# Row products of a batched diagonal in two large VectorE instructions instead of sixteen small ones

## The chip, the cores and the metric

The kernel runs on one core of a Trainium2 chip. The metric is the device time of one execution in microseconds (us), as a median of several executions; the profile describes one of them, and its span is about 2 us shorter than the time. The two kernels are called "before" and "changed".

VectorE (DVE in the profile) is the compute engine that multiplies and sums here. Loads and the output are moved by 16 DMA engines while VectorE works; each moves its part of a transfer in packets, and the trace has 16 landing records for a transfer (768 for the 48 transfers of before). It has landed when the last of the 16 engines has delivered its part: in before the last record of the first y load came at 22.57 us, and the first product started at 22.68.

## The reference

```python
B, N, D = 8, 4096, 512                      # x, y: float32 (B, N, D)
gram = np.matmul(x, y.transpose(0, 2, 1))
diag = np.diagonal(gram, axis1=1, axis2=2)  # = sum over d of x[b,n,d] * y[b,n,d]
diag = diag - diag.max(axis=-1, keepdims=True)
exp = np.exp(diag)
out = exp / exp.sum(axis=-1, keepdims=True) # softmax over the 4096 rows of a batch
```

Only the diagonal is wanted, so the kernel needs one dot product of 512 elements per row. It must read 134.2 MB and does little arithmetic on them.

## The kernel before

A batch has 4096 rows, 32 on each of 128 partitions. It is loaded in two half batches of 16 rows a partition; there are 16 half batches, n = 0 to 15, each with an x and a y tile of 4 MB in a pool of three buffers.

```python
R, H, P = 32, 16, 128                       # rows of a batch and of a half batch on a partition; partitions
io = ctx.enter_context(tc.tile_pool(name="io", bufs=3))

def load(b, r0, parts):                     # x and y on the same queue, piece by piece
    xt = io.tile([P, H, D], f32, ...); yt = io.tile([P, H, D], f32, ...)
    o = 0
    for n in parts:
        nc.sync.dma_start(out=xt[:, o:o+n, :], in_=xv[b, :, r0+o : r0+o+n, :])
        nc.sync.dma_start(out=yt[:, o:o+n, :], in_=yv[b, :, r0+o : r0+o+n, :])
        o += n
    return xt, yt

def dots(b, r0, xt, yt):                    # one instruction for each row
    for k in range(H):
        c = b * R + r0 + k
        nc.vector.scalar_tensor_tensor(out=xt[:, k, :], in0=xt[:, k, :], scalar=1.0,
            in1=yt[:, k, :], op0=mult, op1=mult, accum_out=diag[:, c:c+1])

# softmax(b): 4 VectorE, 2 GpSimd, 1 ScalarE instructions and the output of 16 KB  [cut]

for b in range(B):
    for h in range(2):
        last = b == B - 1 and h == 1
        parts = [8, 4, 2, 1, 1] if last else [H]
        xt, yt = load(b, h * H, parts)
        dots(b, h * H, xt, yt)
    softmax(b)
```

## Time and profile before

| | before |
|---|---|
| time, median (3 runs) | 325.55 us (325.40 to 325.62) |
| span of the profiled run | 323.8 us |
| DMA engines busy | 90% or more from the 2nd to the 38th of 40 slices |
| data moved | 134.2 MB, 415 GB/s over the span |
| VectorE (DVE) busy | 164.4 us, 51% |
| last load has landed | 318.36 us |

These are lines of the page of before: VectorE's busy time; VectorE and the DMA engines in 40 equal slices of the span (a digit is the busy share in tenths); the queues (packets, MB, share); the chain of waits by engine; and the two largest groups of instructions (count, busy us, mean ns, then the idle time before them).

```profile
DVE 164.4 (51%) x544; ACT 4.6 (1%) x17; POOL 6.1 (2%) x20
...
DVE  0019075290944709256191742908348091571994
...
DMA  8999999999999999999999999999999999999980
...
q1 hardware_dynamic: 5760, 134.22, 96.6%
...
q14 instruction: 5, 0.04, 0.0%
...
DMA 82%; DVE 16%; issue 1%; SPq 0%; POOLq 0%; POOL 0%; DVEq 0%
...
L51 DVE SCALAR_TENSOR_TENSOR xt<-xt,yt 128x512 f32<-128x512 f32 x256 | 158.3, 687 | 144.1 <-DMA yt<-in_y_dram 144.1
L51 DVE DVE_READ_ACCUMULATOR xt<-xt,yt 128x1 f32 x256 | 21.1, 82 | 0.0
```

The loads set the time. VectorE waits 144 us for them. A row product leaves two records on VectorE, the product and the read of its accumulator. The 16% of VectorE in the chain is not a bottleneck: it is the link from the release of a buffer to the issue of the next load, and that load then stands in a queue: the one issued at 269.00 us lands 39.28 us later. The end of the chain shows it (start us, length us, what):

```profile
258.72 9.90 DVE xt L51 x32
...
268.63 0.33 SPq L43
268.96 0.04 issue
269.00 39.28 DMA yt<-in_y_dram
...
308.30 10.06 DMA yt<-in_y_dram
318.36 0.03 issue
318.40 0.04 issue
318.45 0.71 DVE xt L51 x2
```

The last y piece lands at 318.36; one row product and a softmax follow, 5.4 us to the end of the span.

**Below the page: an uneven load.** The trace also records, for each transfer, when each of the 16 DMA engines has delivered its part. Below, *lag* is the time of the last of the 16 minus the median of the 16, "middle" is that median; both are worked out from these records. Until 47 us the lag is 0.2 us. Then it rises in steps, and the second slowest engine stays within 0.3 us of the middle in all loads, so it is one engine that falls behind. The steps come where the instruction queue (q14 above) moves a packet of 8 KB; the 32 KB packet of a load that starts as the instruction packet ends takes longer than the usual 1213 ns (the median):

```
before: packets of the instruction queue, and the load packet beside each
 starts at us   takes ns   next 32 KB load packet takes ns   lag afterwards us
    47.4          332              1875                        1.0
   125.0          309              1787                        1.9
   185.5          309              1862                        2.9
   263.0          312              1869                        3.9
   322.7          493              none (the loads are over)
```

The time of an instruction packet and the lengthening of the load packet add up to 0.88 to 0.99 us, about the size of a step. The last load is complete only when the slowest engine is. 15 of 16 engines had ended by about 314.8 us; the kernel waited for the one to 318.36.

### The profile page before, as it was taken

To read this page: it belongs to the slowest core of one execution; us is meant where nothing else is said; L and a number is where in the kernel's file an instruction comes from. 1 tells how busy PE (TensorE), PEld (TensorE's weight loads), DVE (VectorE), ACT (ScalarE), POOL (GpSimd) and SP (SyncE) were. 2 spreads that over 40 slices of the span, in tenths; PEclk is the share of its full clock that TensorE was granted. 3 is DMA by queue.
4 is the path that set the end of the run, shared out by engine and by line. 5 is a ranking of instruction groups with operands and counts; after the bars stand their busy time and mean duration, and the time that the engine had idled before them with its cause. 6 is when DMAs were issued, how large, how long until landed. Compare 5 with 4: busy or idle time off the path is not lost.

```text
span 323.8 us, 727 instructions
## 1 busy us (share of the span) xinstructions
DVE 164.4 (51%) x544; ACT 4.6 (1%) x17; POOL 6.1 (2%) x20
## 2 busy tenths in 40 slices
DVE  0019075290944709256191742908348091571994
ACT  1000000000000000000000000000000000000000
POOL 0000000000000000000000000000000000000000
DMA  8999999999999999999999999999999999999980
GB/s 324 453 401 441 453 410 429 455 409 433 449 397 451 445 401 446 450 398 449 449 397 450 452 393 453 445 397 455 445 397 453 446 394 453 445 397 425 429 319 10
DMA packets 6917, 134.39 MB, mean 415 GB/s; under 512 B 1792, under 2 KB 1792, under 8 KB 2560
## 3 DMA queue, kind: packets, MB, share of 16 engines
q1 hardware_dynamic: 5760, 134.22, 96.6%
q10 hardware_dynamic: 1152, 0.13, 0.3%
q14 instruction: 5, 0.04, 0.0%
HBM read 134.22 MB, written 0.13 MB: 415 GB/s over the span
## 4 chain that ended last, share of the span: by engine, by line
DMA 82%; DVE 16%; issue 1%; SPq 0%; POOLq 0%; POOL 0%; DVEq 0%
DMA yt<-in_y_dram 82%; DVE xt L51 16%; SPq L43 0%; DVE mxp L65 0%; POOLq L114 0%; POOL mx L67 0%; DVE res L79 0%; DVE rc L78 0%; DVEq L51 0%; DVEq L79 0%; POOLq L67 0%
## 5 line engine op out<-in xcount | busy, mean ns | idle before, releaser
L51 DVE SCALAR_TENSOR_TENSOR xt<-xt,yt 128x512 f32<-128x512 f32 x256 | 158.3, 687 | 144.1 <-DMA yt<-in_y_dram 144.1
L51 DVE DVE_READ_ACCUMULATOR xt<-xt,yt 128x1 f32 x256 | 21.1, 82 | 0.0
L67 POOL PARTITION_ALL_REDUCE mx<-mxp x8 | 2.8, 350 | 308.9 <-DVE mxp L65 308.9
L71 ACT ACTIVATE res<-diag,nmx 128x32 f32<-128x32 f32 x8 | 2.6, 321 | 315.2 <-DVE nmx L69 315.2
L78 DVE RECIPROCAL rc<-ssum 128x1 f32<-128x1 f32 x8 | 1.3, 164 | 7.6 <-POOL ssum L76 7.6
L69 DVE TENSOR_SCALAR nmx<-mx 128x1 f32<-128x1 f32 x8 | 1.2, 154 | 4.3 <-POOL mx L67 4.3
L76 POOL PARTITION_ALL_REDUCE ssum<-sump x8 | 3.1, 383 | 5.8 <-ACT res L71 5.8
L79 DVE TENSOR_SCALAR res<-res,rc 128x32 f32<-128x32 f32 x8 | 1.9, 241 | 0.9
L65 DVE TENSOR_REDUCE mxp<-diag 128x1 f32<-128x32 f32 x8 | 1.5, 186 | 0.3
L71 ACT ACTIVATION_READ_ACCUMULATOR res<-diag,nmx 128x1 f32 x8 | 1.5, 186 | 0.0
L71 ACT ACT_TABLE_LOAD x1 | 1.3, 1283 | 0.7 <-PEq L103 0.7
L103 POOL MEMSET const-float32-0.0<- 128x1 f32 x1 | 0.1, 98 | 0.2 <-issue 0.2
L103 POOL MEMSET const-bfloat16-1.0<- 128x1 bf16 x1 | 0.1, 102 | 0.0
L103 POOL MEMSET const-uint8-127<- 128x1 uint8 x1 | 0.1, 101 | 0.0
L103 POOL MEMSET const-float32-1.0<- 128x1 f32 x1 | 0.1, 98 | 0.0
## 6 DMA issues: line engine op xcount, KB each, us to landing
xt<-in_x_dram SPq DMA_DIRECT2D x15, 4096.0 KB, 39.6
yt<-in_y_dram SPq DMA_DIRECT2D x15, 4096.0 KB, 48.9
xt<-in_x_dram SPq DMA_DIRECT2D x1, 2048.0 KB, 34.7
yt<-in_y_dram SPq DMA_DIRECT2D x1, 2048.0 KB, 39.3
xt<-in_x_dram SPq DMA_DIRECT2D x1, 1024.0 KB, 41.3
yt<-in_y_dram SPq DMA_DIRECT2D x1, 1024.0 KB, 43.4
xt<-in_x_dram SPq DMA_DIRECT2D x1, 512.0 KB, 35.5
yt<-in_y_dram SPq DMA_DIRECT2D x1, 512.0 KB, 27.0
```

The costliest lines, as they stand in the source:

```text
L51: nc.vector.scalar_tensor_tensor(out=xt[:, k, :], in0=xt[:, k, :], scalar=1.0, in1=yt[:, k, :], op0=mybir.AluOpType.mult, op1=mybir.AluOpT ...
L65: nc.vector.tensor_reduce(out=mxp, in_=db, axis=mybir.AxisListType.X, op=mybir.AluOpType.max)
L67: nc.gpsimd.partition_all_reduce(out_ap=mx, in_ap=mxp, channels=P, reduce_op=bass_isa.ReduceOp.max)
L69: nc.vector.tensor_single_scalar(out=nmx, in_=mx, scalar=-1.0, op=mybir.AluOpType.mult)
L71: nc.scalar.activation(out=rb, in_=db, func=mybir.ActivationFunctionType.Exp, bias=nmx, scale=1.0, accum_out=sump,)
L76: nc.gpsimd.partition_all_reduce(out_ap=ssum, in_ap=sump, channels=P, reduce_op=bass_isa.ReduceOp.add)
L78: nc.vector.reciprocal(out=rc, in_=ssum)
L79: nc.vector.tensor_single_scalar(out=rb, in_=rb, scalar=rc, op=mybir.AluOpType.mult)
L103: nc = _bacc.Bacc("TRN2", target_bir_lowering=False, num_devices=1)
```

## The change

The intent is fewer, larger VectorE instructions: one product over all 16 rows and one reduction, for the first 13 half batches. The last three stay row by row, where VectorE must be quick, and the second last is loaded in two pieces.

```diff
     def dots(b, r0, xt, yt):
+        c = b * R + r0
+        nc.vector.tensor_tensor(out=xt, in0=xt, in1=yt, op=mybir.AluOpType.mult)
+        nc.vector.tensor_reduce(
+            out=diag[:, c : c + H], in_=xt, axis=mybir.AxisListType.X, op=mybir.AluOpType.add
+        )
+
+    def dots_by_row(b, r0, xt, yt):
         for k in range(H):
             c = b * R + r0 + k
             nc.vector.scalar_tensor_tensor(
@@
-            last = b == B - 1 and h == 1
-            parts = [8, 4, 2, 1, 1] if last else [H]
+            n = 2 * b + h
+            parts = {2 * B - 2: [8, 8], 2 * B - 1: [8, 4, 2, 1, 1]}.get(n, [H])
             xt, yt = load(b, h * H, parts)
-            dots(b, h * H, xt, yt)
+            (dots_by_row if n >= 2 * B - 3 else dots)(b, h * H, xt, yt)
```

## The prediction

> **What bounds it now.** The loads. The page's slice view shows the DMA engines 90% busy or more from the second slice to the last but one, 134.2 MB at 415 GB/s over a 323.8 us span. The chain of waits is 82% "DMA yt"; the 16% of VectorE row products in it is only the link from a buffer's release to the next load's issue, and that load then queues 49 us. VectorE is busy 51%: a half batch lands every 19.4 us, its 16 row products take 9.9 us, a softmax 2.35 us every second half batch. At the end (timeline) the last y piece lands at 318.36, VectorE has then waited 0.58 us, and one row plus a softmax (5.4 us) follow.
>
> **What is less plain.** The DMA records show an uneven load. In each transfer 15 of 16 engines finish within about 0.25 us of each other; the last lags 1.0, 1.9, 2.9 and at the end 3.8 us behind the middle one. The lag steps up at 48, 126, 186 and 264 us, when the instruction queue (5 packets of 8 KB) moves a packet: the 32 KB packet beside it takes 1.8 instead of 1.21 us. I read these as VectorE's instruction fetches: some 130 VectorE records (a row product counts as two) lie between two. [...]
>
> **Removed, added, moved.** In 13 half batches 16 row products become a product and a reduction over 128x8192. [...] VectorE busy rises from 164 to about 260 us. It still fits: two half batches and a softmax are 37.1 us against 38.9 us of loading. A buffer comes free 17.4 instead of 9.9 us after landing, but about 21 us of loads are queued then. None of this is on the critical path.
>
> What is on it: VectorE's records fall from 544 to about 154, so the fetches during the loads fall from four to about one. The slow engine then ends about 1 us instead of 3.8 us behind: gain 2.8 us. Without the second-last half batch in two pieces VectorE could not use this, with its 0.58 us of slack at the end; [8, 8] starts its row products about 9.7 us earlier.
>
> **Predicted: 322.8 us**, range 321.9 to 324.5 (325.55 - 2.8, 0.8% faster). Chances: faster by over 2%: 0.02; within 2%: 0.95; slower by over 2%: 0.03.
>
> **What shows each step.**
> - Product and reduction each about 8.7 us in the groups; VectorE about 80% busy.
> - Instruction queue: 2 packets instead of 5, one of them after the last load.
> - The last y piece lands near 315.6 us, the slowest engine's lag about 1 us; VectorE waits before each last piece.
> - Packets still 1.21 us for 32 KB.
> - Loads issued about 7.5 us later after landing, with no gap in DMA.
>
> **What would make it wrong.** The reduction costs over about 10.5 us: VectorE becomes the bound, slower. The fetches are another engine's, or the lag tracks time: no gain. No fetch before the end: 322. VectorE's long two-input instructions hold back DMA writes: slower.

## The result, and the profile after

| | before | changed |
|---|---|---|
| time, median (4 runs each) | 325.52 us | 323.53 us (323.29 to 323.94) |
| span of the profiled run | 323.8 us | 321.6 us |
| VectorE busy | 164.4 us (51%) | 261.4 us (81%) |
| VectorE records counted as busy | 544 | 154 |
| instruction fetches before the last load | 4 | 1 |
| lag at the last load | 3.75 us | 1.00 us |
| last load has landed | 318.36 us | 316.13 us |

The ratio of the fast runs is 0.994, with a 95% interval of 0.9923 to 0.9958. The gain of 2.0 us is clear of the noise and far below 2%.

The same lines of the page of the changed kernel:

```profile
DVE 261.4 (81%) x154; ACT 4.6 (1%) x17; POOL 6.1 (2%) x20
...
DVE  0019979898998979979799897989979799776494
...
DMA  8999999999999999999999999999999999999991
...
q1 hardware_dynamic: 6048, 134.22, 97.5%
...
q14 instruction: 1, 0.01, 0.0%
...
DMA 63%; DVE 33%; issue 1%; SPq 1%; POOL 1%; ACT 0%; POOLq 0%; DVEq 0%
...
L50 DVE TENSOR_TENSOR xt<-xt,yt 128x8192 f32<-128x8192 f32 x13 | 113.0, 8689 | 34.5 <-DMA yt<-in_y_dram 34.5
L51 DVE TENSOR_REDUCE diag<-xt 128x16 f32<-128x8192 f32 x13 | 112.9, 8686 | 0.4
L58 DVE SCALAR_TENSOR_TENSOR xt<-xt,yt 128x512 f32<-128x512 f32 x48 | 30.0, 687 | 9.9 <-DMA yt<-in_y_dram 9.7
```

VectorE does 97 us more work, and the kernel is faster. The DMA line is as full as it was; the instruction queue has one packet instead of five in the span. The end of the chain, to be held against that of before:

```profile
265.91 8.70 DVE diag L51
274.61 0.02 issue
274.62 0.33 SPq L43
274.95 0.04 issue
275.00 30.96 DMA yt<-in_y_dram
305.95 0.02 issue
305.97 10.16 DMA yt<-in_y_dram
316.13 0.02 issue
316.15 0.71 DVE xt L58 x2
```

The last load lands 2.23 us earlier (318.36 - 316.13). The buffer of n = 12 is released at 274.6 instead of 268.6, and it does no harm: the load issued then still stands 31 us in the queue. VectorE's share of the chain has doubled, to 33%, because a half batch now holds its buffer for 17.4 us of VectorE work instead of 9.9 us and the chain passes through six of them instead of five; it costs no time at the end.

### The profile page after: what moved, and what is told of

It is laid out like the page before. It is cut to its first block, busy times and chain, and to the rows that moved or that the text cites. A ratio compares the mean times of both kernels' runs of the same rounds, so it can differ in the third digit from the quotient of the medians.

```text
span 321.6 us, 345 instructions
## 1 busy us (share of the span) xinstructions
DVE 261.4 (81%) x154; ACT 4.6 (1%) x17; POOL 6.1 (2%) x20
## 4 chain that ended last, share of the span: by engine, by line
DMA 63%; DVE 33%; issue 1%; SPq 1%; POOL 1%; ACT 0%; POOLq 0%; DVEq 0%
DMA yt<-in_y_dram 63%; DVE xt L50 16%; DVE diag L51 16%; SPq L43 1%; POOL mx L74 0%; POOL ssum L83 0%; DVE mxp L72 0%; DVE xt L58 0%; ACT res L78 0%; DVE rc L85 0%; POOLq L121 0%; SPq L44 0%; DVE res L86 0%; DVE nmx L76 0%; DVEq L50 0%
## 5 line engine op out<-in xcount | busy, mean ns | idle before, releaser
L50 DVE TENSOR_TENSOR xt<-xt,yt 128x8192 f32<-128x8192 f32 x13 | 113.0, 8689 | 34.5 <-DMA yt<-in_y_dram 34.5
L51 DVE TENSOR_REDUCE diag<-xt 128x16 f32<-128x8192 f32 x13 | 112.9, 8686 | 0.4
L58 DVE SCALAR_TENSOR_TENSOR xt<-xt,yt 128x512 f32<-128x512 f32 x48 | 30.0, 687 | 9.9 <-DMA yt<-in_y_dram 9.7
L58 DVE DVE_READ_ACCUMULATOR xt<-xt,yt 128x1 f32 x48 | 3.9, 82 | 0.0
```

The lines of the kernel that those rows point to most:

```text
L50: nc.vector.tensor_tensor(out=xt, in0=xt, in1=yt, op=mybir.AluOpType.mult)
L51: nc.vector.tensor_reduce(out=diag[:, c : c + H], in_=xt, axis=mybir.AxisListType.X, op=mybir.AluOpType.add)
```

## The experiments

Every experiment was timed over five rounds against the kernel before, except one look (all_large); no_split has four times on record. "Fetches" are the 8 KB packets of the instruction queue before the last load has landed; lag and middle are of the last load, from the landing records of the profiled run. ScE is ScalarE. Times are medians, so a row joins a median time to the landings of one run, which can be a slower one (no_split_again's profiled run took 323.56 us). all_large and the two cuts are told below; the kernel before had 325.51, 325.56, 325.61 and 325.57 us.

```
kernel           time us   fetches      lag    middle   last load
before           325.52    4            3.75   314.60   318.36
rows_pieces      326.60    4            3.68   314.60   318.27
rows_pad1        326.24    4            3.75   314.59   318.34
pad_vector       325.36    3            3.01   314.60   317.61
six_large        324.73    3            2.82   315.21   318.03
changed          323.53    1            1.00   315.13   316.13
after_again      323.43    1            0.92   315.07   315.99
pad_scalar       323.33    1 + 2 ScE    1.27   314.56   315.84
no_split         322.98    1            0.97   314.44   315.40
no_split_again   322.96    1            0.92   315.13   316.05
two_by_row       322.79    1            0.99   314.54   315.52
```

My theory: what the change saves is VectorE's instruction fetches, each of which holds back one and the same DMA engine by about 1 us. The main rivals: the pieces 8, 8 make the gain, or the larger form of the work does.

### pad_vector: put the fetches back, leave everything else

```diff
+    pad = persist.tile([P, 256], f32, name="pad")
+    for i in range(256):
+        nc.vector.memset(pad[:, i : i + 1], 0.0)
     for b in range(B):
         for h in range(2):
```

> The changed kernel plus 256 one-element memsets on VectorE before the first product, when VectorE waits for the first load anyway. Theory (what slows the last load is the number of VectorE instruction fetches): two more 8 KB packets of the instruction queue in the first 20 us, three in all before the last load; the slowest DMA engine's lag over the middle one at the last load rises from 1.0 to about 2.9 us; 325.4 us, so the whole gain is gone though the products, reductions and loads are those of the changed kernel. Rival (the gain comes from the form of the VectorE work or from the pieces 8, 8): no change, 323.5 us, lag 1.0.

Measured: 325.36 us, ratio to before 0.9994 (0.9981 to 1.0006). The gain of 2.0 us is gone but for 0.15 us. The instruction queue on its page and the end of its chain:

```profile
q14 instruction: 3, 0.02, 0.0%
```

```profile
307.53 10.07 DMA yt<-in_y_dram
317.61 0.02 issue
317.63 0.71 DVE xt L58 x2
```

The two new packets came at 6.4 and 12.0 us, while VectorE had no other work. The memsets were over at 10.05 us, the first product started at 24.5, and the products and reductions took 8689 and 8686 ns as in the changed kernel. VectorE itself stood still for 0.4 us after 61 memsets and for 1.6 us after 189, that is 128 memsets apart, with no wait that the profile shows; this fits fetches of its own. Its timeline:

```profile
0.79 1.75 DVE L91 MEMSET pad<- 128x1 f32 x61 [0.79 <-PEq L113]
2.91 3.64 DVE L91 MEMSET pad<- 128x1 f32 x128 [0.37 <-issue]
8.13 1.92 DVE L91 MEMSET pad<- 128x1 f32 x67 [1.59 <-issue]
```

Still the last load lands 1.5 us later (317.61 against 316.13), 300 us after the memsets. The middle engine ended even earlier, at 314.60 instead of 315.13; only the lag carries the delay over. It rose from 1.00 to 3.01 us, and it was 2.05 us from the first load on. This is the experiment that settles the mechanism. Beside the kernel before there is one fetch less, and the last load lands 0.75 us earlier (317.61 against 318.36); the time hides this, because from the end of the span to the end of the time 2.2 to 2.4 us went by in its runs and 1.7 to 1.8 in those of before (see the end term below).

### pad_scalar: the same number of instructions on ScalarE

```diff
+    pad = persist.tile([P, 256], f32, name="pad")
+    zero = persist.tile([P, 1], f32, name="zero")
+    nc.vector.memset(zero, 0.0)
+    for i in range(256):
+        nc.scalar.copy(out=pad[:, i : i + 1], in_=zero)
```

> The changed kernel plus 256 one-element copies on ScalarE at the start. If fetches of all engines load the same DMA engine: two more fetches, lag 2.9 us at the last load, 325.4 us. If each engine's fetches have their own DMA engine: the largest lag is about 2.0 us, the second largest about 1.0 us, time about 324.5 us. If only VectorE's fetches count: 323.5.

Measured: 323.33 us, with two more fetches at 9.7 and 21.2 us. The load packets beside them took 1459 and 1594 ns, less than the 1875 ns beside VectorE's. After these two the lag was 1.3 us; when VectorE's one fetch came at 241.6 us the largest lag stayed at 1.3 and the second largest rose to 0.9 us. So they are two different DMA engines, and only the slower of the two counts. The time is nearer to "no change" than to my 324.5. A ScalarE fetch cost about 0.55 us of lag and not 1, so the lag at the last load was 1.27 us instead of my 2.0; and what follows the end of the span took 1.9 to 2.0 us instead of the changed kernel's 2.3. Why it was shorter is open.

### six_large: half the change

```diff
-            (dots_by_row if n >= 2 * B - 3 else dots)(b, h * H, xt, yt)
+            (dots_by_row if n >= 6 else dots)(b, h * H, xt, yt)
```

> The products of the first 6 half batches in large instructions, the other 10 by row; pieces as in the changed kernel. Theory: about 395 VectorE records, so three fetches before the last load; lag 2.9 us; 324.8 to 325.4 us. Rival (gain in proportion to the half batches changed, 6 of 13): 324.6 us with a lag of about 2.7; only the number of fetches, whole ones, tells the two apart. Rival (pieces alone): 323.5.

Measured: 324.73 us, three fetches (145.1, 222.7, 293.6 us), lag 2.82. It is just under the 324.8 to 325.4 that I expected. Its profiled run was one with a late middle (see below), and 324.73 us does not tell a whole number of fetches from a gain in proportion. The count and the lag in the trace do support the theory; the time doesn't decide.

### no_split and no_split_again: without the pieces 8, 8

```diff
-            parts = {2 * B - 2: [8, 8], 2 * B - 1: [8, 4, 2, 1, 1]}.get(n, [H])
+            parts = {2 * B - 1: [8, 4, 2, 1, 1]}.get(n, [H])
```

> The changed kernel with the second-last half batch in one piece as before. What the prediction said: VectorE, with 0.58 us of slack at the end, can't use the earlier landing: about 325.0 us. Rival: that half batch lands earlier too, by the same reduced lag, so VectorE's tail moves along with it: 323.4 us, with under 1 us of wait before the last row.

Measured: 322.98 us, faster than the changed kernel. The claim of the prediction fell. The end of its chain:

```profile
305.27 10.14 DMA yt<-in_y_dram
315.40 0.03 issue
315.43 0.02 DVEq L58
315.45 0.04 issue
315.50 0.71 DVE xt L58 x2
```

VectorE had still waited 0.57 us before that last row. Since 0.5 us between calls proves little, both were run again on one chip:

> The changed kernel unaltered, beside the one without the pieces. It shows whether its 323.53 us and its middle DMA engine's later end hold. Theory: one fetch at 241 us, lag 1.0; 323.3 to 323.5 us.

> The changed kernel with the second-last half batch in one piece, on the same chip as after_again. If the pieces 8, 8 cost something: 0.2 to 0.6 us faster than after_again. If the earlier difference was one of chips or of runs: equal within 0.2 us.

Measured: 323.43 us (323.38 to 323.87) and 322.96 us (322.70 to 323.56). The medians differ by 0.47 us in the same direction as before, 0.55; the ranges overlap. The pieces don't help and appear to cost about 0.5 us. About 0.1 us of it can be reckoned from packets: a 32 KB packet took 1218.5 ns on average in before, two of 16 KB 2 x 613.5 = 1227 ns in the changed kernel, and 256 such pairs on 16 engines make 0.14 us. By the medians another 0.25 to 0.4 us lies after the end of the span: 2.3 us went by there in every run of the changed kernel and 1.8 to 2.1 without the pieces. Why is open.

### rows_pieces: only the pieces 8, 8, all products by row

```diff
-            last = b == B - 1 and h == 1
-            parts = [8, 4, 2, 1, 1] if last else [H]
+            n = 2 * b + h
+            parts = {2 * B - 2: [8, 8], 2 * B - 1: [8, 4, 2, 1, 1]}.get(n, [H])
```

> The kernel before with only the pieces 8, 8 added; every product by row. Theory: four fetches, lag 3.8 us, no gain: 325.5 to 325.9 us. Rival (the pieces make the gain): 323.5.

Measured: 326.60 us, ratio to before 1.0027 (1.0015 to 1.004). The rival falls: the pieces alone give no gain. But it is 1.0 us slower, which I had not expected, though its last load landed at 318.27, as in before. In its trace the fifth fetch starts at 322.2 us instead of 322.7, that is, during the last output, and the last output's lag is 0.92 us instead of 0.09. In before the packets of that output had ended at 322.65 us, and the fetch at 322.72 missed them by 0.07 us. Its VectorE has one record more than before (579 against 578, waits included). That made a new theory, with a test:

### rows_pad1: the kernel before with one memset more

```diff
+    pad = persist.tile([P, 256], f32, name="pad")
+    for i in range(1):
+        nc.vector.memset(pad[:, i : i + 1], 0.0)
     for b in range(B):
         for h in range(2):
```

> The kernel before with one memset on VectorE at its start and nothing else. It asks why rows_pieces was 1.0 us slower than the kernel before with its loads ending at the same time. Theory: rows_pieces has one VectorE record more (579 against 578), so the fifth fetch comes 0.5 us earlier, while the last output is written, and holds back one engine's part of it. Then one memset does the same: 326.3 to 326.7 us, lag of the last output 0.9 us instead of 0.1. Rival (the pieces cost it): 325.5.

Measured: 326.24 us, ratio to before 1.0019 (1.0006 to 1.0031). One instruction that is over in the first microseconds makes the kernel 0.6 us slower. The fifth fetch moved to 322.4 us, and the last output's lag rose to 0.81 us; the four earlier fetches and the lag of the loads are those of before. So a fetch on the last output is shown to cost about 0.6 us here, 0.1 us under what I expected. It accounts for 0.6 of the 1.0 us of rows_pieces; where the other 0.4 us comes from is not shown (the two profiled runs, 326.41 and 326.31 us, are nearly alike).

### all_large: the last three half batches in large instructions too

```diff
-            (dots_by_row if n >= 2 * B - 3 else dots)(b, h * H, xt, yt)
+            dots(b, h * H, xt, yt)
```

> The changed kernel with the last three half batches in large instructions too. The last load then lands as before, near 316 us, but VectorE begins the last product after it, 8.7 + 8.7 us, and may still be working on the half batch before: 335 to 341 us. It shows that the larger VectorE cost is hidden only as long as another load follows.

Measured in one look (a single run, state unknown): 339.9 us. The end of its chain:

```profile
305.72 9.89 DMA yt<-in_y_dram
315.62 0.02 issue
315.64 8.70 DVE xt L50
324.34 0.02 issue
324.37 8.70 DVE diag L51
333.06 0.02 issue
333.09 0.20 DVE mxp L72
```

The last load lands at 315.62, and then 17.4 us of VectorE work follow instead of 0.7. So the larger VectorE cost was hidden here only where another load followed.

### cut_120 and cut_early: take work from the slow engine

If the slow engine could be given less, the last 1 us of lag would go. My guess was that a transfer of 120 partitions is spread over 15 engines and leaves one out; which one, I did not know. The traces of cut_120 and cut_early bear out the number: the transfers of 120 and of 8 partitions have 15 and 8 landing records (a whole load has 16), besides one that comes within 1 us of the issue.

Both are changes to no_split; the lines below are those of cut_120. In cut_early the half batch n = 5 is also loaded in pieces of 15 and 1 rows.

```diff
-            nc.sync.dma_start(out=xt[:, o : o + n, :], in_=xv[b, :, r0 + o : r0 + o + n, :])
-            nc.sync.dma_start(out=yt[:, o : o + n, :], in_=yv[b, :, r0 + o : r0 + o + n, :])
+            cuts = [0, 120, P] if o == 14 else [0, P]     # cut_early: the same for row 15 of n = 5
+            for p, q in zip(cuts, cuts[1:]):
+                nc.sync.dma_start(out=xt[p:q, o:o+n, :], in_=xv[b, p:q, r0+o : r0+o+n, :])
+                nc.sync.dma_start(out=yt[p:q, o:o+n, :], in_=yv[b, p:q, r0+o : r0+o+n, :])
```

> The kernel without the pieces 8, 8, with the two loads of row 14 of the last half batch cut into partitions 0 to 119 and 120 to 127. It is a guess: if 120 partitions are spread over 15 engines [...] and the one left out is the one that VectorE's fetches slow, that engine has 1.4 us less to do and the lag at the last load goes from 1.0 to about 0.2 us: 322.4 us. If another engine is left out: lag still 1.0, about 323.1 us.

> The kernel without the pieces 8, 8, with one row of the sixth half batch (n = 5) loaded by itself, cut into partitions 0 to 119 and 120 to 127; in the middle of the run, where 20 us of loads are queued, unlike cut_120. If the engine left out by the 120 partitions is the one of VectorE's fetches: no lag after the fetch at 241 us, 322.2 to 322.5 us. If it is another one: lag 1.0 to the end, 323.0 to 323.2 us.

Measured: 325.15 and 324.80 us, both slower than no_split. It was the wrong engine. In cut_early one engine delivers its part of the last loads 0.6 us ahead of all others, and one still lags by 1.0 us. In cut_120 the slow one is among the eight of the 8-partition transfer: the last of its eight landings is 1.1 to 1.2 us behind the seventh. Why these two are some 2 us slower than no_split was not settled, but in cut_early the trace shows where: its middle engine is 0.25 us behind that of no_split before the cut row (100.23 against 99.98), 1.57 us behind just after it (130.73 against 129.16) and as far behind at the last load (315.98 against 314.44). Only the loads of the cut half batch and the next x lie between, so the cut cost the middle engine about 1.3 us. What in it does so is open.

### two_by_row: a better version

```diff
-            (dots_by_row if n >= 2 * B - 3 else dots)(b, h * H, xt, yt)
+            (dots_by_row if n >= 2 * B - 2 else dots)(b, h * H, xt, yt)
```

(on top of no_split)

> The kernel without the pieces 8, 8, with only the last two half batches by row; the third last in large instructions too. It is a search for a better version. By the numbers of all_large and no_split VectorE ends the third last half batch and its softmax at about 296.0 us, just as the second last lands (296.2), so nothing is lost at the end; the fetch stays one, since it comes at 241 us. Theory: 322.8 to 323.1 us, like no_split, lag 1.0. If fewer VectorE records alone helped in proportion, 30 fewer would be worth about 0.2 us: 322.7.

Measured: 322.79 us (322.66 to 323.02), ratio to before 0.9913 (0.9899 to 0.9927), the fastest of all, though within noise of no_split. The timeline shows how tight the hand-over is (start us, length us, engine, line, operation); in no_split VectorE had time to spare here:

```profile
295.51 0.16 DVE L85 RECIPROCAL rc<-ssum 128x1 f32<-128x1 f32 x1 [0.96 <-POOL ssum L83]
...
295.78 0.24 DVE L86 TENSOR_SCALAR res<-res,rc 128x32 f32<-128x32 f32 x1
295.93 0.69 DVE L58 SCALAR_TENSOR_TENSOR xt<-xt,yt 128x512 f32<-128x512 f32 x1
```

## Why the prediction was right or wrong

- **The bound and the hidden work: right.** VectorE rose to 81% busy, and product and reduction took 8689 and 8686 ns; the prediction's 17.4 us per half batch was my estimate for the two together. The page of before gives about the same by an estimate of its own: a reduction of 32 elements took 186 ns there and a row product of 512 took 687, so 1.04 ns for each further element, if all these instructions lie on one line, and 8.7 us for 8192. The loads stayed the bound. The slower DMA writes that the prediction names last are not seen: the usual 32 KB packet took 1213 ns (median) with VectorE 51% and 81% busy.
- **Fetches: right in number and effect.** Four fell to one, and the lag from 3.75 to 1.00 us, the predicted 2.8. pad_vector shows that this is the cause. The page shows one instruction packet and not the two I named, since the second (323.3 us) came after the span of 321.6 us. The one fetch came at 241 us, when 62 VectorE records (waits included) stood before it; in before it was 53 before the first, and 113 to 140 lay between one packet and the next.
- **The size: 2.0 us instead of 2.8.** Two terms were missing from the sum "325.55 - 2.8". The first is the end. From the end of the span to the end of the time 1.7 to 1.8 us went by in all recorded runs of before, and 2.3 us in all nine runs of the changed kernel. From the landing of the last output it was 2.61 us (325.61 - 323.00) and 3.24 (323.94 - 320.70) in the profiled runs. It was 3.2 in pad_vector too, where a fetch follows the last output as in the changed kernel, and 2.6 in two_by_row, which has none. But no_split, with such a fetch, had 2.8 and 2.9, and all_large, without, 3.0. This term stays open. It takes 0.5 to 0.6 us from the 2.8 in every run.
- **The second missing term is the middle engine, and it is one of some runs only.** In the profiled run of the changed kernel the middle ended at 315.13 instead of 314.60, so 0.53 us of the 2.75 were taken back and the landing gained 2.23. That run, 323.94 us, was the slowest of its four; the profiled runs of after_again, six_large and no_split_again, also with a late middle (315.07 to 315.21), were the slowest or second slowest of theirs. So this term says little about the median: after_again's three runs near 323.4 us are what 325.5 - 2.75 + 0.6 gives without it. It is not due to the change: no_split had a middle of 314.44 in one profiled run and 315.13 in another. In the four profiled runs with a late middle a 32 KB packet took 1216.9 to 1217.8 ns on average, without the few that took over 1400 ns; in the others 1215.0 to 1215.8, except cut_early with 1216.8. Two ns on 224 packets of an engine are 0.45 us. What makes the packets slower in some runs was not found.
- **"Without the second-last half batch in two pieces VectorE could not use this": wrong.** I took the 0.58 us of slack as fixed. But the second-last half batch lands earlier by nearly the same reduced lag, so VectorE's tail moves with the landings and keeps its slack, 0.57 us in no_split. The pieces were not needed, and they appear to cost 0.5 us. That the predicted time held all the same owes nothing to this step.
- **"VectorE waits before each last piece": wrong.** It waited 4.72 us before the first piece of the last half batch and 0.50 us before the last row, and hardly between.
- **Loads issued later without a gap: right.** See the chains (274.6 against 268.6).

## What to carry to other kernels

In a kernel bound by loads, the number of instructions can matter even on an engine that has time to spare: here, with VectorE 51% busy, the lag of one DMA engine grew from 0.2 to 3.75 us over four packets of the instruction queue, and two packets more, from the changed kernel to pad_vector, made 1.8 us of time. Look at how evenly the DMA engines finish, and count the packets of the instruction queue; the one engine that was held back four times set the end, at 318.36 us against 314.60 for the middle. Large instructions with more total work were free while another load followed (97 us more of VectorE work in a kernel 2.0 us faster) and expensive after the last one (339.9 us in all_large, a single run, against 323.53). A slack seen at the end of a chain must be worked out anew when everything ahead of it moves: it was 0.58 us in before and still 0.57 us in no_split, whose last load landed 2.96 us earlier.
